# A two-block transformer kernel on one core: weight sums of the seven-product feed-forward made a step ahead, modulation loads, residual loads and stores moved

## The chip, the core and the metric

The kernel runs on one NeuronCore of a Trainium2 chip. Five engines work from queues of their own, each in the order written: PE (TensorE, matrix products), DVE (VectorE), ACT (ScalarE), POOL (GpSimd) and SP (which only issues transfers here). The metric is the device time of one execution in microseconds (us), the median of three runs.

## What is computed

Two blocks over 1024 tokens of width 1024, all in float32. The first is attention and spatial gating and then a gated feed-forward of width 2816; the second takes a modulation vector from `c`, projects, and goes through window attention, a short convolution and a mixture of 16 experts. What the change touches is the end of the first block and the modulation:

```python
xn = rms_norm(x, ffn_norm_g[l])
gate, up = jnp.split(xn @ w_gate_up[l], 2, axis=-1)
x = x + (jax.nn.silu(gate) * up) @ w_down[l]
...
mod = jnp.einsum('bd,de->be', jax.nn.silu(c), w_mod[layer]) + b_mod[layer]
mod_c = jnp.einsum('d,de->e', jax.nn.silu(c_ctx), w_mod[layer]) + b_mod[layer]
```

and, in the second block, the projection `hx @ w_in`, part of which is made in the same way.

## The kernel before

Activations stand transposed, 128 features by 1024 tokens to a tile. A float32 product is three matmuls of rounded parts (`mm3`, L65 to L67): high by high, low by high, high by low. `split` (L58, L59) makes the parts: ACT copies to the high part, DVE subtracts it to get the low one.

The hidden width of the feed-forward is 22 strips of 128 (FF = 22, `f` counts them). Strips 0 to 2 are made plainly. For `f` from 3 (NCL) on, the gate's and the up weights' column strip and the two halves of the tokens form a 2 x 2 problem that `quads` does with seven products instead of eight: seven sums of weights, seven sums of activations (`SEVX`, made beforehand), 12 matmuls each, and an evacuation `after[i]` behind each product. `after[1]` and `after[5]` end in a gate: a sum on DVE (`plus`, L326), a multiplication by the norm's factors on POOL (`times`, L1182) and SiLU on ACT (L1186). `after[4]` and `after[6]` end in `times` alone. `hidden_out` (L1137, L1138) then multiplies gate and up on DVE and stores the strip to DRAM from POOL's queue (L1139); it is put off (`flush`) to the head of the next step.

The weights come through class `Weights`. `fill` issues loads on SP (L132) into four staging tiles; `seven` lists the seven sums of a pair (a, b): a11, a12, s2 = a21 + a22 - a11, s1 = a21 + a22, a11 - a21, a12 - s2, a22. Four of these are POOL operations: `make2` makes s1 (L153) and s2 (L154), `make3` a11 - a21 (L158), `make4` a12 - s2 (L162). `conv` calls the sum, then `split`s it. `get` hands out the next prepared pair of parts and first calls `conv` until five are ready (`ahead` is 4 in the steps, 2 in the last). So what `conv` issues for product i + 4 stands, on every engine, in front of the evacuation of product i.

Beside this, the modulation: `w_mod` is 48 pieces of 512 KB (12 column strips s of 4 pieces). `mods` first sums a finished strip with matmuls against ones (`mod_sum`, L1108, L1109), then `mod_load` asks for a piece and at once accumulates it on DVE (L1097, L1099): four operations for s < 4, where both vectors are needed, two after that. One call stands at the end of each step, the rest stands between the feed-forward's halves and in the second half.

The second half multiplies the strips by `w_down` in five parts (`parts`: 5, 5, 4, 4, 4). `h_load` reads strips back into two buffers (`phr`) and `h_split` splits them; the residual `x1` is read back from `d_xs` on SP (L1249) ahead of the first part, and `columns_k` adds each product to it (L1257). The second block's projection uses `quads` again, 20 times (`quads_`, L1490 on).

```python
        def get(self):
            self.prime(1 + self.ahead)
            return self.ready.popleft()
...
            wh, wl = W.get()
            bk.append(psb.tile([P, 512], F32, name="b"))
            for k in range(4):
                mm3(bk[i], wh[:, k, :], wl[:, k, :], xh_(k), xl_(k), k == 0, k == 3)
            after[i]()
            if i in mid:
                mid[i]()
```

## Time and profile before

| | before |
|---|---|
| median of 3 runs | 3119.93 us (3118.93 to 3121.84) |
| the profiled execution | 3115.53 us |
| its span | 3113.6 us |
| mean granted clock of PE | 0.959 of full |
| PE busy | 2873.2 us, 92% |
| DVE, ACT, POOL busy | 2035.0, 1415.2, 813.1 us |

The span is the time from the first to the last instruction that the profiler records; the 1.9 us more of the execution lie around it. "Busy" of PE is modelled from the starts of the matmuls. The feed-forward in sevens goes from about 560 to 1071 us of the span, its second half to about 1350, the second block's steps of seven from about 1520 to 1890.

### The profile page before, as it was taken

To read this page: it belongs to the slowest core of one execution; us is meant where nothing else is said; L and a number is where in the kernel's file an instruction comes from. 1 tells how busy PE (TensorE), PEld (TensorE's weight loads), DVE (VectorE), ACT (ScalarE), POOL (GpSimd) and SP (SyncE) were. 2 spreads that over 40 slices of the span, in tenths; PEclk is the share of its full clock that TensorE was granted. 3 is DMA by queue.
4 is the path that set the end of the run, shared out by engine and by line. 5 is a ranking of instruction groups with operands and counts; after the bars stand their busy time and mean duration, and the time that the engine had idled before them with its cause. 6 is when DMAs were issued, how large, how long until landed. Compare 5 with 4: busy or idle time off the path is not lost.

```text
span 3113.6 us, 37585 instructions
## 1 busy us (share of the span) xinstructions
PE 2873.2 (92%) x13715; PEld 2378.2 (76%) x13715; DVE 2035.0 (65%) x2925; ACT 1415.2 (45%) x2241; POOL 813.1 (26%) x789
## 2 busy tenths in 40 slices
PE   9999999888878699999999998999999879999997
PEld 7987878666666578788788887777778758888885
DVE  4346845655555445687666663589942389999998
ACT  4346933222222211252223232488831268888886
POOL 2201312244434300033444431133221311121113
PEclk9999999988888899999999999999999989999998
DMA  5120133122222364334222236200054489999997
GB/s 193 45 72 15 47 137 109 61 81 81 81 75 74 107 210 161 123 100 144 75 86 87 86 109 240 92 14 15 35 187 153 156 291 370 377 377 372 377 377 282
DMA packets 303880, 472.76 MB, mean 152 GB/s; under 512 B 15260, under 2 KB 144000, under 8 KB 303568
## 3 DMA queue, kind: packets, MB, share of 16 engines
q1 hardware_dynamic: 282368, 395.46, 37.0%
q0 software_dynamic: 19840, 73.85, 6.8%
q8 instruction: 108, 1.77, 0.2%
q10 hardware_dynamic: 1488, 1.06, 0.1%
q14 instruction: 76, 0.62, 0.1%
HBM read 396.35 MB, written 73.96 MB: 151 GB/s over the span
## 4 chain that ended last, share of the span: by engine, by line
PE 68%; DVE 11%; issue 7%; POOL 6%; ACT 5%; DMA 2%; SPq 0%; POOLq 0%; ACTq 0%; DVEq 0%
PE b L67 19%; PE b L65 19%; PE b L66 19%; DVE acc L1099 1%; PE pt L1726 1%; DVE wl L59 1%; ACT wh L58 1%; PE b L2107 1%; POOL c L1182 1%; PE po L1756 1%; POOL wst L158 1%; POOL u L1182 1%; PE po L1757 1%; POOL ws L154 1%; POOL ws L153 1%
## 5 line engine op out<-in xcount | busy, mean ns | idle before, releaser
L59 DVE TENSOR_TENSOR wl<-wst,wh 128x1024 fp32r<-128x1024 f32 (+2 forms) x677 | 740.2, 1121 | 280.0 <-ACT wh L58 269.7
L58 ACT ACTIVATE wh<-wst 128x1024 fp32r<-128x1024 f32 (+2 forms) x677 | 610.3, 922 | 529.8 <-POOL wst L158 187.5
L65 PE MATMUL b<-wh,a 128*128 128x512 f32 x768 | 302.0, 393 | 0.2 <-ACT a L58 0.2
L66 PE MATMUL b<-wl,a 128*128 128x512 f32 x768 | 299.4, 390 | 0.8 <-DVE wl L59 0.8
L67 PE MATMUL b<-wh,a 128*128 128x512 f32 x768 | 299.4, 390 | 0.4 <-DVE a L59 0.4
L2149 POOL DMA_INDIRECT d_x<-b,idxT x15 | 65.8, 4388 | 469.9 <-DVE b L2143 469.9
L67 PEld LDWEIGHTS b<-wh,a 128*128 128x128 f32 x768 | 144.2, 188 | 30.9 <-DVE a L59 1.0
L66 PEld LDWEIGHTS b<-wl,a 128*128 128x128 f32 x768 | 144.5, 188 | 30.5 <-DVE wl L59 1.6
L65 PEld LDWEIGHTS b<-wh,a 128*128 128x128 f32 x768 | 144.5, 188 | 29.6 <-ACT a L58 0.7
L59 DVE TENSOR_TENSOR wl<-ws,wh 128x512 fp32r<-128x512 f32 x78 | 53.6, 690 | 157.3 <-ACT wh L58 157.3
L65 PE MATMUL b<-xn,wh 128*128 128x512 f32 x368 | 145.6, 396 | 5.7 <-ACT xn L58 4.8
L67 PE MATMUL b<-xn,wl 128*128 128x512 f32 x368 | 145.1, 394 | 2.6 <-DVE wl L59 2.6
L65 PE MATMUL b<-hH,wh 128*128 128x512 f32 x352 | 143.0, 406 | 4.5 <-ACT hH L58 4.5
L66 PE MATMUL b<-xn,wh 128*128 128x512 f32 x368 | 145.1, 394 | 0.5 <-DVE xn L59 0.5
L66 PE MATMUL b<-hL,wh 128*128 128x512 f32 x352 | 141.5, 402 | 1.2 <-DVE hL L59 1.2
L67 PE MATMUL b<-hH,wl 128*128 128x512 f32 x352 | 140.8, 400 | 0.0
L58 ACT ACTIVATE wh<-ws 128x512 fp32r<-128x512 f32 x78 | 47.5, 622 | 177.5 <-POOL ws L154 134.4
L65 PE MATMUL b<-t3h,wh 128*128 128x512 f32 x76 | 46.5, 611 | 87.6 <-ACT wh L58 87.6
L1099 DVE SCALAR_TENSOR_TENSOR acc<-mw,s,acc 128x512 f32<-128x512 f32 x112 | 95.7, 864 | 29.3 <-DMA mw<-in_w_mod_dram 26.5
L1707 DVE CUSTOM_DVE_ANT_0 sm<-sp,mk,nsk 128x640 f32<-128x640 f32 (+1 forms) x128 | 107.1, 838 | 0.6 <-PE sp L1696 0.3
L1744 DVE TENSOR_TENSOR pl<-pt,ph 128x512 fp32r<-128x512 f32 x152 | 102.0, 686 | 7.9 <-ACT ph L1736 7.3
L1714 ACT ACTIVATE sm<-sm,tn 128x640 f32<-128x640 f32 (+1 forms) x128 | 103.0, 805 | 0.5 <-DVE tn L1707 0.3
(668 smaller groups left out, 7622.1 us busy)
## 6 DMA issues: line engine op xcount, KB each, us to landing
wst<-in_w_exp_gate_dram SPq DMA_DIRECT2D x128, 512.0 KB, 10.8
wst<-in_w_exp_up_dram SPq DMA_DIRECT2D x128, 512.0 KB, 10.8
wst<-in_w_exp_down_dram SPq DMA_DIRECT2D x128, 512.0 KB, 10.8
wst<-in_w_in_dram SPq DMA_DIRECT2D x74, 512.0 KB, 4.0
mw<-in_w_mod_dram SPq DMA_DIRECT2D x48, 512.0 KB, 5.0
wst<-in_w_gate_up_dram SPq DMA_DIRECT2D x44, 512.0 KB, 4.1
d_h<-hr POOLq DMA_DIRECT2D x22, 512.0 KB, 2.9
hr<-d_h SPq DMA_DIRECT2D x22, 512.0 KB, 4.1
```

Of the source, the lines that this page charges most:

```text
L58: act(h, src, AF.Copy)
L59: DVE.tensor_tensor(l, src, rd(h), op=OP.subtract)
L65: PE.matmul(ps, lh, rh, start=start, stop=False)
L66: PE.matmul(ps, lh, rl, start=False, stop=False)
L67: PE.matmul(ps, ll, rh, start=False, stop=stop)
L153: POOL.tensor_tensor(s1[0], a21, a22, op=OP.add)
L1099: DVE.scalar_tensor_tensor(a, t[:, kk, :], sc, a, op0=OP.mult, op1=OP.add)
L1182: POOL.tensor_tensor(x, x, rsb[:, cs], op=OP.mult)
L1707: DVE.tensor_tensor_reduce(sms[n][:, :nk], sps.pop(n)[:, 256:256 + nk], (mk if i else mk0)[:, :nk], -0.125, nsk[:, hd:hd + 1], op0=OP.add, ...
L1714: act(sms[n][:, :nk], sms[n][:, :nk], AF.Exp, bias=m, scale=-1.0, accum_out=s)
L1744: DVE.tensor_tensor(pl, pt, rd(ph), op=OP.subtract)
L2149: nc.gpsimd.indirect_dma_start(out=d_x2, out_offset=bass.IndirectOffsetOnAxis(ap=idxT[:, e:e + 1], axis=0), in_=y, in_offset=None, compute ...
```

## The change

The three POOL operations s1, s2 and a11 - a21 become one function `make` in a queue `sums`; `presum` runs the next one. In the steps of the feed-forward it is called behind the third product for the next step's pair; in the first step, and wherever it was not called, `conv` calls it at the second sum. The second block's steps do the same. `mod_load` only loads; `mod_use` accumulates at the next call (`mod_next`). In the steps this stands behind the second product, and up to f = 10 behind the fourth as well, until 24 pieces are loaded; the other 24 are spread over the second half. The store of a strip is put off to behind the third product of the next step. The first two strips are read back in the last step, into a third buffer. The residual is read back on POOL's queue in two halves.

```diff
+        def presum(self):
+            if self.sums:
+                self.sums.popleft()()
...
-            def make2():
+            def make():
                 for x, n in ((s1, "ws1"), (s2, "ws2")):
                     x.append(self.tmp.tile([P, 512], F32, name=n).rearrange("p (k n) -> p k n", n=P))
                 POOL.tensor_tensor(s1[0], a21, a22, op=OP.add)
                 POOL.tensor_tensor(s2[0], s1[0], a11, op=OP.subtract)
-                return s2[0]
-
-            def make3():
                 POOL.tensor_tensor(a21, a11, a21, op=OP.subtract)
-                return a21
...
+            def second():
+                if not s1:
+                    self.presum()
+                return s2[0]
+            self.sums.append(make)
...
-    phr = pool(es_hr, "phr", 2)
+    phr = pool(es_hr, "phr", 3)
...
         nc.sync.dma_start(t, wsrc(w_mod_2[0], k, 2, s * 512, 512))
+        mwq.append((s, k, t))
+
+    def mod_use(s, k, t):
...
-        nc.gpsimd.dma_start(d_h[f], h)
+        stored.append(lambda: nc.gpsimd.dma_start(d_h[f], h))
...
+    def mod_next(left=0):
+        if mwq:
+            mod_use(*mwq.popleft())
+        if len(modq) > left:
+            mod_load(*modq.popleft())
+
+    def early(f):
+        if f < FF - 1:
+            W.presum()
+        else:
+            for _ in range(2):
+                h_load(next(nxt))
...
+    def mods1():
+        if modr:
+            mod_sum(modr.popleft())
+        mod_next(24)
...
-                  lambda s, b: (times(plus(s, s, b), h0), su.update(s=s)), lambda s, b: times(plus(c2, s, b), h1))
+                  lambda s, b: (times(plus(s, s, b), h0), su.update(s=s)), lambda s, b: times(plus(c2, s, b), h1),
+                  {1: mods1, 2: lambda: (stores(), early(f)), **({3: mods1} if f < NCL + 8 else {})})
             flush.append(lambda hr_=hr_, c1=c1, c2=c2, su=su, f=f: hidden_out(hr_, c1, c2, su, f))
-            mods()
-            if f == NCL:
-                mods()
...
-            if not i and not c0:
-                for k in range(KD):
-                    nc.sync.dma_start(x1[k], d_xs[k])
+            if not i:
+                for k in range(c0, c0 + 4):
+                    nc.gpsimd.dma_start(x1[k], d_xs[k])
...
-                mid={(p0, 3): (lambda p0=p0: step(p0)) for p0 in range(0, n, 2)} if c0 else ())
+                mid={(p0, c): (lambda p0=p0: step(p0)) if c0 and c == 3 else mod_next for p0 in range(0, n, 2) for c in (1, 3) if i or c0})
             if c0:
                 step(n)
-            for _ in range(4):
-                mods()
+            while modr:
+                mod_sum(modr.popleft())
...
-              lambda s, b: plus(c2, s, b))
+              lambda s, b: plus(c2, s, b), {2: W.presum})
```

On POOL, one step of the feed-forward before, from the gate multiplication of the second product to that of the next step's (c, u and s are the halves that are multiplied, ws the two sums of weights, wst a staging tile):

```order
L1182 TENSOR_TENSOR c_5117<-c_5117,s_3907 128x512
L153 TENSOR_TENSOR ws_5216<-wst 128x512
L154 TENSOR_TENSOR ws_5217<-ws_5216,wst 128x512
L1182 TENSOR_TENSOR u<-u,s_3907 128x512
L1182 TENSOR_TENSOR s<-s,s_3907 128x512
L1139 DMA d_h_4597<-hr 128x1024
L158 TENSOR_TENSOR wst<-wst 128x512
L162 TENSOR_TENSOR wst<-wst,ws_5217 128x512
L1182 TENSOR_TENSOR c_5275<-c_5275,s_3907 128x512
```

and in the changed kernel (L158 and L159 make the sums, L160 the difference, L164 the last sum, L1227 multiplies, L1151 stores):

```order
L1227 TENSOR_TENSOR c_5271<-c_5271,s_3907 128x512
L1151 DMA d_h_4597<-hr 128x1024
L158 TENSOR_TENSOR ws_5339<-wst 128x512
L159 TENSOR_TENSOR ws_5340<-ws_5339,wst 128x512
L160 TENSOR_TENSOR wst<-wst 128x512
L1227 TENSOR_TENSOR c_5272<-c_5272,s_3907 128x512
L1227 TENSOR_TENSOR u<-u,s_3907 128x512
L1227 TENSOR_TENSOR s<-s,s_3907 128x512
L164 TENSOR_TENSOR wst<-wst,ws_5340 128x512
```

The store and three weight operations now stand in one piece between the step's two first gate multiplications, and one weight operation stands at its end.

On DVE, the end of a step and the head of the next before (wl is the low part of a prepared weight, acc the modulation's accumulator, hr the hidden strip):

```order
L326 TENSOR_TENSOR s<-s,b 128x512
L1099 SCALAR_TENSOR_TENSOR acc_6342<-mw,s_70,acc_6342 128x512 x2
L1099 SCALAR_TENSOR_TENSOR acc_6345<-mw,s_70,acc_6345 128x512 x2
L1137 TENSOR_TENSOR hr<-u,c_6353 128x512
L1138 TENSOR_TENSOR hr<-s,c_6352 128x512
L59 TENSOR_TENSOR wl<-wst,wh 128x512 x2
L326 TENSOR_TENSOR c_6503<-s,b 128x512
```

and in one of the changed kernel's steps up to f = 10:

```order
L335 TENSOR_TENSOR s<-s,b 128x512
L1149 TENSOR_TENSOR hr<-u,c_5753 128x512
L1150 TENSOR_TENSOR hr<-s,c_5752 128x512
L59 TENSOR_TENSOR wl<-wst,wh 128x512 x2
L335 TENSOR_TENSOR c_5923<-s,b 128x512
L1111 SCALAR_TENSOR_TENSOR acc_5855<-mw,s_70,acc_5855 128x512 x2
L1111 SCALAR_TENSOR_TENSOR acc_5858<-mw,s_70,acc_5858 128x512 x2
L59 TENSOR_TENSOR wl<-wst,wh 128x512
L321 TENSOR_TENSOR s<-s,b 128x512
L59 TENSOR_TENSOR wl<-wst,wh 128x512
L322 TENSOR_TENSOR u<-s,b 128x512
L1111 SCALAR_TENSOR_TENSOR acc_5855<-mw,s_70,acc_5855 128x512 x2
```

The accumulations have gone from the end of the step to behind the second evacuation, and a second group of four stands behind the fourth.

## Rows read from the trace of the kernel before

**Rows 1.** Stretches: start:end, length, busy PE, PEld, DVE, ACT, POOL, clock, DMA.
```profile
600.00:627.20 27.20, 21.95 (x85) 17.28 (x84) 14.27 (x21) 5.71 (x11) 11.18 (x9) 0.88 0.24 78
1530.00:1700.00 170.00, 170.00 (x752) 140.77 (x751) 111.32 (x148) 52.45 (x87) 79.53 (x59) 1.00 0.26 81
```

**Rows 2.** Timeline, PE: start, duration; first matmul of two last products, f = 3, 21.
```profile
580.01 0.39 PE L65 MATMUL b<-t4h,wh 128*128 128x512 f32 x1
...
1065.73 0.39 PE L65 MATMUL b<-t4h,wh 128*128 128x512 f32 x1
```

**Rows 3.** The chain that ended last, 600 to 660 us: start, duration, what.
```profile
600.80 0.69 DVE c L326
...
602.83 5.67 issue
...
609.78 1.30 POOL ws L153
...
612.47 0.64 ACT wh L58
...
618.31 0.67 DVE acc L1099
...
622.72 0.61 DVE hr L1138
...
624.22 1.27 POOL wst L158
...
628.01 0.69 DVE c L326
```

**Rows 4.** Timeline, PE, one step's fifth product; in brackets idle before.
```profile
626.21 0.80 PE L65 MATMUL b<-t3h,wh 128*128 128x512 f32 x1 [5.25 <-ACT wh L58]
...
628.35 0.63 PE L66 MATMUL b<-t3l,wh 128*128 128x512 f32 x1
628.77 0.63 PE L67 MATMUL b<-t3h,wl 128*128 128x512 f32 x1
```

**Rows 5.** Waits, 600 to 1060 us: us in total, times, longest.
```profile
DVE wl L59 <- ACT wh L58: 219.1, 69, 4.7
ACT wh L58 <- POOL wst L158: 133.8, 17, 8.5
...
ACT wh L58 <- POOL ws L154: 126.0, 17, 7.4
```

**Rows 6.** Timeline, DVE and POOL, the same step.
```profile
604.04 0.69 DVE L59 TENSOR_TENSOR wl<-wst,wh 128x512 fp32r<-128x512 f32 x1 [2.56 <-ACT wh L58]
...
618.23 3.89 DVE L1099 SCALAR_TENSOR_TENSOR acc<-mw,s,acc 128x512 f32<-128x512 f32 x4
618.39 1.73 POOL L1182 TENSOR_TENSOR s<-s,s 128x512 f32<-128x512 f32 x1 [2.59 <-DVE s L326]
```

**Rows 7.** Line 1099, 570 to 1060 us: duration in ns, least/median/most.
```profile
L1099 DVE SCALAR_TENSOR_TENSOR acc<-mw,s,acc x61: 739/752/1666, 589.2 to 1050.9; 128x512 f32<-128x512 f32 x61
```

**Rows 8.** Timeline, DVE and POOL at two places in the second block's steps.
```profile
1628.19 4.06 DVE L59 TENSOR_TENSOR wl<-wst,wh 128x512 fp32r<-128x512 f32 x2 [3.51 <-ACT wh L58]
...
1630.06 1.63 POOL L154 TENSOR_TENSOR ws<-ws,wst 128x512 f32<-128x512 f32 x1
...
1832.86 0.55 POOL L1539 DMA_DIRECT2D d_ga<-g  x1 [10.78 <-ACT g L1536]
...
1833.12 0.69 DVE L59 TENSOR_TENSOR wl<-ws,wh 128x512 fp32r<-128x512 f32 x1 [1.22 <-ACT wh L58]
```

**Rows 9.** Timeline, PE, between the feed-forward's halves.
```profile
1077.05 1.87 PE L1108 MATMUL b<-ones,acc 128*128 128x1 f32 x8 [8.44 <-DVE acc L1099]
...
1086.02 0.80 PE L65 MATMUL b<-hH,wh 128*128 128x512 f32 x1 [4.49 <-ACT hH L58]
```

**Rows 10.** Waits of PE, 1066 to 1365 us.
```profile
PE b L1108 <- DVE x L1257: 7.7, 3, 3.0
```

**Rows 11.** The page's DMA issues: KB each, us to landing.
```profile
wst<-in_w_gate_up_dram SPq DMA_DIRECT2D x44, 512.0 KB, 4.1
```

More of the change, by code (lines that the diff above doesn't have):

```diff
@@ L83, in __init__ @@
             self.ready = deque()
-            self.wait, self.spare, self.tmp = [], [], None
+            self.wait, self.spare, self.sums, self.tmp = [], [], deque(), None
             if hl:
@@ L163, in make4 @@
                 return a12
-            return [(f, n, True) for f, n in ((lambda: a11, 0), (lambda: a12, 0), (make2, 0), (lambda: s1[0], 0), (make3, 0),
-                                              (make4, 0), (lambda: a22, 2))]
+            def second():
[3 more added lines that the diff above has]
+            self.sums.append(make)
+            return [(f, n, True) for f, n in ((lambda: a11, 0), (lambda: a12, 0), (second, 0), (lambda: s1[0], 0),
+                                              (lambda: a21, 0), (make4, 0), (lambda: a22, 2))]
         def conv(self):
@@ L1138, in hidden_out, with stores, h_load @@
         DVE.tensor_tensor(h[:, h0], su["s"], c1, op=OP.mult)
-        nc.gpsimd.dma_start(d_h[f], h)
+        stored.append(lambda: nc.gpsimd.dma_start(d_h[f], h))
+    mwq, stored = deque(), deque()
+    def stores():
+        while stored:
+            stored.popleft()()
+    def mod_next(left=0):
[9 more added lines that the diff above has]
+                h_load(next(nxt))
+    hraw = deque()
+    nxt = iter(range(FF))
+    def h_load(f):
+        hraw.append(phr.tile([P, T], F32, name="hr"))
+        nc.sync.dma_start(hraw[-1], d_h[f])
+    def mods1():
+        if modr:
+            mod_sum(modr.popleft())
+        mod_next(24)
     for f in range(FF):
@@ L1200, in fused @@
     W.spare.clear()
-    while modq and modq[0][1]:
-        mod_load(*modq.popleft())
-    while modr:
-        mod_sum(modr.popleft())
+    stores()
+    assert len(modq) == 24 and not modr and not mwq
     es_mo.close()
@@ L1216, in fused @@
     pmo = pool(es_mo, "pmo2", 2)
-    hraw = deque()
-    def h_load(f):
-        hraw.append(phr.tile([P, T], F32, name="hr"))
-        nc.sync.dma_start(hraw[-1], d_h[f])
     def h_split():
@@ L1227, in h_split @@
         return h, l
-    nxt = iter(range(FF))
     def h_in():
@@ L1236, in h_in @@
         return r
-    for _ in range(2):
-        h_load(next(nxt))
     hTs = []
@@ L1246, in fused @@
         for c0 in (0, 4):
-            if not i and not c0:
-                for k in range(KD):
-                    nc.sync.dma_start(x1[k], d_xs[k])
+            if not i:
+                for k in range(c0, c0 + 4):
+                    nc.gpsimd.dma_start(x1[k], d_xs[k])
             hn, nn = [], parts[i + 1][1]
             def step(p0):
-                while len(hn) < min(nn, p0 + 2 + 5 - n):
+                while len(hn) < min(nn, p0 + 5 - n):
                     hn.append(h_in())
@@ L1258, in fused @@
                 x1[c0 + c][:, hf * 512:(hf + 1) * 512], x1[c0 + c][:, hf * 512:(hf + 1) * 512], ps, op=OP.add), 2,
-                mid={(p0, 3): (lambda p0=p0: step(p0)) for p0 in range(0, n, 2)} if c0 else ())
+                mid={(p0, c): (lambda p0=p0: step(p0)) if c0 and c == 3 else mod_next for p0 in range(0, n, 2) for c in (1, 3) if i or c0})
             if c0:
                 step(n)
-            for _ in range(4):
-                mods()
+            while modr:
+                mod_sum(modr.popleft())
         hTs = hn
-    while modq or modr:
-        mods()
+    while modq or mwq:
+        mod_next()
+    while modr:
+        mod_sum(modr.popleft())
     es_mo.close()
@@ L1509, in fused @@
               lambda s, b: act(g[:, h0], plus(s, s, b), AF.Sigmoid),
-              lambda s, b: act(g[:, h1], plus(g2, s, b), AF.Sigmoid))
+              lambda s, b: act(g[:, h1], plus(g2, s, b), AF.Sigmoid), {2: W.presum})
         nc.gpsimd.dma_start(d_y[j], y)
```

## The prediction

> **What bounds the kernel now.** I read the stretches first, then the order of waits inside one of them. Where the second block projects with seven products per step, TensorE is busy for all of 170.00 us and runs 752 matmuls, 0.226 us each, at clock 1.00 [rows 1]. Where the first block's feed-forward does the same seven products, it is busy 21.95 of 27.20 us, and the granted clock is 0.88. So the second place shows what the first could be: a step has 7 x 12 = 84 matmuls, 84 x 0.2267 = 19.05 us at full clock. It takes 27.0 us on average: the last product of step f = 3 begins at 580.01, that of f = 21 at 1065.73, so 485.7 us for 18 intervals [rows 2].
>
> What takes the other 8 us is seen in the chain of waits of one step [rows 3]. Within 27.21 us (600.80 to 628.01) it hardly touches TensorE: it runs DVE, POOL, ACT, DVE, POOL and round again, because each engine takes its instructions in the order written and each evacuation stands behind a preparation for the next step. TensorE runs ahead on prepared weights and then waits 5.25 us for the fifth product's. After that wait its matmuls start 0.42 us apart instead of 0.23 [rows 4]: the records show the lower of its two clock levels, 1.2 instead of 2.4 GHz. A dozen matmuls at the lower level cost 12 x 0.2 = 2.4 us. 19.05 + 5.25 + 2.4 is 26.7, the step nearly whole. The waits say what is late: ACT waited 133.8 us for POOL's a21 difference (L158) and 126.0 us for its two sums (L154) in 17 steps [rows 5].
>
> **The change, part by part: the step.** I take the links of [rows 3] that leave the chain.
> - Sums L153 and L154 stood between the gate of the second half and the third evacuation: 609.78 to 612.47, 2.7 us. They are now made in the step before, after its third product.
> - The four modulation accumulations stood before the hidden rows were finished: 618.31 to 622.04 (L1137's 0.68 us before L1138), 3.7 us. They now stand after the second product.
> - The store: from the end of L1138 at 623.33 to L158 at 624.22, 0.9 us. It moves past the third product of the next step, where the rows are long finished.
> - L158 itself, 1.3 us, goes with the sums.
>
> Together 8.6, which leaves 18.6 us. Three things are added.
> - POOL now has store, two sums and difference in one piece (0.55 + 1.30 + 1.30 + 1.27 = 4.4 us, by [rows 3, 8]) between its two gate multiplications. POOL was free there (602.83, 5.67 us [rows 3]), so POOL is not late. DVE may be: its conversions stand in that same stretch (from 604.04 [rows 6]), and two conversions that met POOL's sums took 4.06 us instead of some 1.3, while POOL's L154 took 1.63 instead of 1.30 [rows 3, 8]. An issue of a store does not do that: a conversion that began inside one took 0.69 us [rows 8]. So the cost lies between 0 and the three operations' 3.85 us. Both sides gave way in the row, so I take the middle, 1.9 us.
> - The copy of the next step's first product overwrites the half that the last hidden multiplication reads, and it is now the next link: ACT's 0.6 us, against a POOL operation (L162, 1.3 us) that may leave the chain. Between -0.6 and +0.6; I take +0.3, since the copy is certain and the other is not.
> - The accumulations. From f = 11 on there are two a step. DVE is idle for 2.56 us in front of the conversion at 604.04 [rows 6]; two at 0.75 us [rows 7] fit: nothing. In f = 3 to 10 there are two groups of four. The first has 3.0 us for 2.56 of idle time: 0.4. The second, after the fourth product, lies on the chain: 3.0. Each group meets a POOL operation, as the group at 618.23 did (3.89 us for 3.0 [rows 6]): 2 x 0.9.
>
> So a late step costs 18.6 + 1.9 + 0.3 = 20.8 us, above TensorE's 19.05 (bounds 19.05, and 18.6 + 3.85 + 0.6 = 23.1). An early step costs 20.8 + 0.4 + 3.0 + 1.8 = 26.0, hardly less than now. The last step prepares only two products ahead; I leave it at 27. Intervals: 7 early, 10 late, 1 last: 182 + 208 + 27 = 417 against 485.7, **-69 us**.
>
> The bound of the wait for POOL is where a rule of the skill says more than a row. In 1628 to 1632 both engines were held in turn and both lost time [rows 8]. The Trainium skill, "SBUF — State Buffer", section "Who interferes with whom", says that a DVE instruction with two SBUF inputs and a GpSimd instruction that reads SBUF exclude each other for a whole instruction, the one that issues first winning. The rows agree on the exclusion, but show turns taken and not one side always losing. By the rule in full, with all 3.85 us in DVE's way, a late step would be 22.8 and an early one 28.0, the sum -35 instead of -69 and the time 3078 us.
>
> **The other parts.** Between the two halves of the feed-forward TensorE waits 8.44 us for an accumulation and 4.49 us for a hidden row [rows 9]. The accumulation is gone from there, and the first two rows are asked for in the last step, into a third buffer. What remains is their split behind the last hidden multiplications, about 6 us, an estimate: each strip is two halves of 0.64 us on ACT (L58) and two of about 0.6 on DVE (as L1138) [rows 3], so two strips take 5 us, and DVE's queue adds some 1: **-7 us**, between 0 and -13. In the second half three sums of the modulation waited 7.7 us for an evacuation [rows 10]; in the change the sums still follow the evacuations and directly follow their last accumulation, so I take nothing (between -7.7 and +5). Asking for the modulation matrix a step ahead removes waits of DVE, which sets no end there.
> At nothing: the residual's eight loads go from SP's queue to POOL's, whose issues take 0.55 us [rows 8] and stand in an idle POOL, and their tiles are needed some 27 us later by the first evacuations; without that cover they would cost 8 x 0.55 = 4.4 us. The sums made ahead in the second block's steps: TensorE is never idle there [rows 1], so nothing can be won, and the loss is covered as long as that chain stays under 19.05 us. The matrix loads now stand in front of the weight loads in SP's queue, one issue each; a pair of weights is asked for more than a step before its use.
>
> Sum: -69 - 7 = -76. The profiled execution took 3115.53 us, 4.4 less than the median of 3119.93. 3115.5 - 76 + 4.4 = **3044 us**.
>
> **Rivals.**
> - *Port and TensorE alone bind.* If the serial chain no longer closes, only two sums are left: TensorE's 19.05, and the operations that exclude each other. Early: POOL 8 x 1.28 = 10.2, DVE's nine conversions and hidden multiplications 9 x 0.61 (L1138's share in [rows 3]) and eight accumulations 8 x 0.75 [rows 7], 11.5: together 21.7. Late: 10.2 + 7.0 = 17.2, under 19.05. 7 x 21.7 + 10 x 19.05 + 27 = 369, so -117 - 7: 2996 us. For it: 170 us at full TensorE in the same kind of step [rows 1]. Against it: those steps have five or six POOL operations, these eight, and every evacuation here passes through POOL and ACT. Chance 0.14. The early step of this rival is the one that the Trainium skill's exclusion rule (same page and section) would give by itself.
> - *The POOL block lies wholly on DVE's path.* Late steps at their upper bound, 23.1, early ones as much longer, 28.3, nothing won between the halves: 198 + 231 + 27 = 456, -30: 3090 us. For it: 4.06 us for two conversions. Chance 0.17.
> - *Slower: DVE's waiting stays.* DVE waited 219.1 us for ACT in 17 steps, 12.9 us each [rows 5], and ACT's order is unchanged: its conversions still stand behind the gates. If that waiting stays whole, an early step is the old one with four more accumulations and one more turn at POOL, 27.2 + 3.9 + 1.3 = 32.4, and a late one 27.2 - 1.9 + 1.3 = 26.6: 227 + 266 + 27 = 520, +34 - 7: 3147 us. It decides once less than 27/18 = 1.5 us of the 12.9 goes. Against it: most of that waiting is ACT's own waiting for POOL, 133.8 + 126.0 us over 17 steps, and both of those operations now come a step earlier. Chance 0.06.
> - *It does not do what it says.* The sums made ahead wait for weights that have not landed, POOL's queue stands still behind them, and the step keeps its 27 us; only the 7 us are won, 3113 us, not told from no change. Chance 0.03: the loads landed 4.1 us after their issue [rows 11], which comes a step early.
>
> **How the numbers follow.** My forecast has 0.60. A measurement of this kernel can tell 0.2%, about 6 us, from no change. Faster by more: 0.60 + 0.14 + 0.17 = 0.91. Within: 0.03. Slower: 0.06. The range goes from 2985, which takes in most of the first rival, to 3100, which takes in most of the second; left out are the last two (0.09) and the edges of the first two (0.1).
>
> **What would show it.** Right: evenly spaced steps of about 21 us from f = 11 on with clock near 1.00; early steps near 26, uneven, with TensorE waiting at the sums of the modulation (L1120), which its queue now meets in the middle of a step; conversions on DVE lengthened above 1 us where POOL's three operations stand; the PE wait of 8.44 us gone. In pairs of early steps TensorE runs one at 19 us on its lead and pays in the next; if the lower clock follows such waits, a few us are added. Wrong: late steps at 19.05 (the chain is broken, first rival) or above 23; early steps above 28; or a stretch behind the feed-forward that grows by what was won.

## The result, and the profile after

The changed kernel takes 3027.24 us (median of 4 runs, 3026.69 to 3028.96) against 3120.89 us (4 runs, 3118.93 to 3122.38): a ratio of 0.9701, 95% interval 0.9684 to 0.9718, 93.7 us less. The profiled executions, 3115.53 and 3026.69 us, are 88.8 us apart. The forecast was 76 us less in the profiled execution and 3044 us for the median; of the gap of 17 us, 13 lie in the stages below and 4 in the median, which lies 0.6 us above the profiled execution here and lay 4.4 above it before.

In the changed kernel PE is busy for 2842.8 us of the span (94%), DVE for 2093.8, ACT for 1414.8 and POOL for 851.4 us.

The stages answer to [rows 1, 2]. The first matmuls of the seventh product at f = 3 and f = 21 (timeline of PE: start, duration):

```profile
580.08 0.39 PE L65 MATMUL b<-t4h,wh 128*128 128x512 f32 x1
...
990.49 0.39 PE L65 MATMUL b<-t4h,wh 128*128 128x512 f32 x1
```

That is 410.4 us for 18 intervals, against 485.7. The single ones come to 19.0, 35.7, 19.0, 32.7, 19.0, 32.4 and 19.0 us (f = 3 to 10), then 208.8 us for ten, then 24.7. Stretches of the seven early and the ten late intervals (length, busy PE, PEld, DVE, ACT, POOL, granted clock, DMA):

```profile
580.08:757.00 176.92, 151.58 (x637) 124.61 (x636) 140.36 (x169) 39.31 (x70) 88.90 (x63) 0.90 0.31 99
757.00:965.79 208.79, 199.57 (x874) 161.31 (x872) 152.34 (x188) 55.37 (x99) 123.09 (x89) 0.99 0.30 98
```

In the early steps DVE is busy 140 of 177 us, in the late ones TensorE 200 of 209. The waits in the last 17 intervals answer to [rows 5]:

```profile
DVE wl L59 <- ACT wh L58: 70.2, 42, 3.0
...
PE b L1120 <- DVE acc L1111: 23.9, 6, 6.5
ACT wh L58 <- POOL ws L159: 23.4, 17, 1.5
```

DVE's waiting for ACT's high parts fell from 219.1 us to 70.2, ACT's for POOL's weight operations from 133.8 + 126.0 to 23.4. New is TensorE's wait at the sums of the modulation. Its timeline at one of them, in an early step (in brackets the idle time before):

```profile
673.83 1.87 PE L1120 MATMUL b<-ones,acc 128*128 128x1 f32 x8 [6.24 <-DVE acc L1111]
```

Between the halves TensorE now waits 2.13 and 3.99 us where it waited 8.44, 0.76, 4.49 and 0.47 [rows 9]:

```profile
995.50 0.50 PE L65 MATMUL b<-hH,wh 128*128 128x512 f32 x1 [2.13 <-ACT hH L58]
...
999.99 0.80 PE L66 MATMUL b<-hL,wh 128*128 128x512 f32 x1 [3.99 <-DVE hL L59]
```

And in the second half (waits of PE; [rows 10] had 7.7 us, three times):

```profile
PE b L1120 <- DVE x L1288: 4.3, 1, 4.3
PE b L66 <- DVE hL L59: 4.0, 1, 4.0
PE b L1120 <- DVE acc L1111: 3.4, 1, 3.4
PE b L65 <- DVE x L1288: 2.3, 2, 1.2
```

The sums' waiting is as long as before, 4.3 + 3.4 us in two waits; 2.3 us in front of products of hidden strips, for DVE's additions to the residual (L1288), are new.

### Where the time of one step goes now

A late step on DVE, then on POOL (start, duration, operation; in brackets the idle time before and what ended it):

```profile
921.20 2.45 DVE L1111 SCALAR_TENSOR_TENSOR acc<-mw,s,acc 128x512 f32<-128x512 f32 x2
924.32 1.20 DVE L59 TENSOR_TENSOR wl<-wst,wh 128x512 fp32r<-128x512 f32 x1 [0.68 <-ACT wh L58]
925.44 0.67 DVE L321 TENSOR_TENSOR s<-s,b 128x512 f32<-128x512 f32 x1
926.04 1.18 DVE L59 TENSOR_TENSOR wl<-wst,wh 128x512 fp32r<-128x512 f32 x1
...
927.74 1.18 DVE L59 TENSOR_TENSOR wl<-wst,wh 128x512 fp32r<-128x512 f32 x1
...
929.55 0.69 DVE L335 TENSOR_TENSOR c<-s,b 128x512 f32<-128x512 f32 x1
930.16 0.68 DVE L59 TENSOR_TENSOR wl<-ws,wh 128x512 fp32r<-128x512 f32 x1
...
934.47 0.69 DVE L59 TENSOR_TENSOR wl<-ws,wh 128x512 fp32r<-128x512 f32 x1 [3.03 <-ACT wh L58]
...
937.54 1.76 DVE L1150 TENSOR_TENSOR hr<-s,c 128x512 f32<-128x512 f32 x1 [1.18 <-POOL s L1227]
```

```profile
921.36 1.74 POOL L1227 TENSOR_TENSOR c<-c,s 128x512 f32<-128x512 f32 x1 [3.16 <-DVE c L335]
...
923.65 1.31 POOL L158 TENSOR_TENSOR ws<-wst 128x512 f32<-128x512 f32 x1
925.04 1.63 POOL L159 TENSOR_TENSOR ws<-ws,wst 128x512 f32<-128x512 f32 x1
926.63 1.75 POOL L160 TENSOR_TENSOR wst<-wst 128x512 f32<-128x512 f32 x1
...
937.47 1.30 POOL L164 TENSOR_TENSOR wst<-wst,ws 128x512 f32<-128x512 f32 x1
```

The step repeats every 20.6 us. The two accumulations stand where DVE would wait for POOL's and ACT's gate anyway, and cost POOL's multiplication 0.45 us (1.74 for 1.29). The three conversions that meet POOL's L158 to L160 take 1.20, 1.18 and 1.18 us instead of 0.69, which is 1.5 us. `hidden_out`'s last multiplication, which meets L164, takes 1.76 instead of 0.69. Between the conversions stands a sum that reads PSUM (L321) and is not lengthened.

The rows give the manner of it. L1150 begins at 937.54, while L164 runs to 937.47 + 1.30 = 938.77, and ends 0.53 us after that. The conversion of 924.32 ends 0.56 us after L158 (924.96), that of 926.04 0.55 us after L159 (926.67). So whichever of the two comes second waits until the other's instruction has ended, and the price is what is left of it. The Trainium skill, "SBUF — State Buffer", section "Who interferes with whom", states that a DVE instruction with two SBUF inputs contends with a GpSimd instruction that reads SBUF. The rows agree: L59 and L1150 have both inputs in SBUF, L321 has one in PSUM.

An early step, the first and the second group of four accumulations on DVE; then POOL:

```profile
697.28 6.00 DVE L1111 SCALAR_TENSOR_TENSOR acc<-mw,s,acc 128x512 f32<-128x512 f32 x4
...
706.71 2.98 DVE L1111 SCALAR_TENSOR_TENSOR acc<-mw,s,acc 128x512 f32<-128x512 f32 x4
```

```profile
697.44 1.73 POOL L1227 TENSOR_TENSOR c<-c,s 128x512 f32<-128x512 f32 x1 [3.16 <-DVE c L335]
...
699.72 1.31 POOL L158 TENSOR_TENSOR ws<-wst 128x512 f32<-128x512 f32 x1
701.11 1.63 POOL L159 TENSOR_TENSOR ws<-ws,wst 128x512 f32<-128x512 f32 x1
```

The first group meets the gate multiplication and the two sums of weights and takes 6.00 us; the second meets nothing and takes 2.98.

### The profile page after: what moved, and what is told of

It is laid out like the page before. It is cut to its first block, busy times and chain, and to the rows that moved or that the text cites. A ratio compares the mean times of both kernels' runs of the same rounds, so it can differ in the third digit from the quotient of the medians.

```text
span 3024.9 us, 37545 instructions
## 1 busy us (share of the span) xinstructions
PE 2842.8 (94%) x13715; PEld 2366.9 (78%) x13715; DVE 2093.8 (69%) x2925; ACT 1414.8 (47%) x2241; POOL 851.4 (28%) x797
## 4 chain that ended last, share of the span: by engine, by line
PE 46%; DVE 5%; ACT 2%; DMA 2%; issue 2%; POOL 1%; POOLq 0%; SPq 0%; DVEq 0%; ACTq 0%
PE b L67 13%; PE b L66 13%; PE b L65 13%; PE pt L1760 1%; PE b L2141 1%; PE po L1790 1%; DVE pl L1778 1%; DVE wl L59 1%; DVE sm L1741 1%; PE po L1791 1%; DVE qs L1645 1%; DMA z<-d_y 1%; PE b L1983 0%; DMA ot<-d_o 0%; PE sp L1730 0%
## 5 line engine op out<-in xcount | busy, mean ns | idle before, releaser
L59 DVE TENSOR_TENSOR wl<-wst,wh 128x1024 fp32r<-128x1024 f32 (+2 forms) x677 | 768.9, 1163 | 209.3 <-ACT wh L58 201.4
L1111 DVE SCALAR_TENSOR_TENSOR acc<-mw,s,acc 128x512 f32<-128x512 f32 x112 | 114.5, 1031 | 23.8 <-DMA mw<-in_w_mod_dram 21.6
L59 DVE TENSOR_TENSOR wl<-ws,wh 128x512 fp32r<-128x512 f32 x78 | 53.5, 688 | 79.8 <-ACT wh L58 79.8
L1227 POOL TENSOR_TENSOR c<-c,s 128x512 f32<-128x512 f32 x38 | 63.2, 1662 | 148.6 <-DVE c L335 139.1
L1760 PE MATMUL pt<-ident,sm 128*128 128x128 f32 x608 | 90.8, 277 | 8.0 <-DVE qs L1645 7.6
```

The lines of the kernel that those rows point to most:

```text
L59: DVE.tensor_tensor(l, src, rd(h), op=OP.subtract)
L1111: DVE.scalar_tensor_tensor(a, t[:, kk, :], sc, a, op0=OP.mult, op1=OP.add)
L1227: POOL.tensor_tensor(x, x, rsb[:, cs], op=OP.mult)
L1760: PE.transpose(pt[:, hh * P:(hh + 1) * P], sms[4 * u + hh][:, kb * P:(kb + 1) * P], ident)
```

## The experiments

Every run is set beside the changed kernel by stages, all from the first and last matmuls of a product: "steps" from the seventh product of f = 3 to that of f = 21, "between" from there to the first matmul on a hidden strip, "half" from there to the start of the last one, "rest" from there to the span's end. The code of the last is the same in all but u_rest and no_sums; it varies by some us, more in one_group, split_group and units3. What lies before the steps varies between 575 and 581 us. The ratio of each kernel is to runs of the one before that were made beside it (medians of 3118.71 to 3120.89 us).

| kernel | median | ratio to before, 95% | steps | between | half | rest |
|---|---|---|---|---|---|---|
| before | 3120.89 | | 485.7 | 13.0 | 274.3 | 1760.5 |
| changed | 3027.24 | 0.9684 to 0.9718 | 410.4 | 5.0 | 270.0 | 1759.4 |
| u_sums | 3078.38 | 0.9841 to 0.9877 | 458.0 | 5.0 | 270.4 | 1762.9 |
| u_store | 3038.93 | 0.9720 to 0.9759 | 416.6 | 5.0 | 269.8 | 1762.6 |
| u_mods | 3044.32 | 0.9736 to 0.9769 | 422.8 | 4.9 | 271.0 | 1763.2 |
| u_h | 3042.26 | 0.9733 to 0.9768 | 410.3 | 10.5 | 277.9 | 1761.0 |
| u_rest | 3024.83 | 0.9689 to 0.9722 | 410.0 | 5.0 | 269.9 | 1759.1 |
| late_sum | 3028.18 | 0.9685 to 0.9718 | 409.2 | 5.0 | 270.2 | 1760.7 |
| no_sums | 2991.82 | 0.9574 to 0.9608 | 377.8 | 5.0 | 270.7 | 1761.0 |
| one_group | 3044.39 | 0.9739 to 0.9773 | 409.8 | 5.0 | 280.8 | 1769.0 |
| split_group | 3011.39 | 0.9639 to 0.9673 | 378.4 | 4.2 | 281.0 | 1767.2 |
| units | 3005.17 | 0.9617 to 0.9649 | 386.3 | 4.2 | 270.7 | 1762.9 |
| units3 | 3080.15 | 0.9852 to 0.9902 | 383.4 | 6.6 | 342.8 | 1766.3 |
| units_last | 3004.07 | 0.9621 to 0.9647 | 381.9 | 6.7 | 269.2 | 1764.1 |

### Undoing one part: the sums ahead, the store, the accumulations

```diff
# u_sums
 def early(f):
-        if f < FF - 1:
-            W.presum()
-        else:
+        if f == FF - 1:
# u_store, in hidden_out
-        stored.append(lambda: nc.gpsimd.dma_start(d_h[f], h))
+        nc.gpsimd.dma_start(d_h[f], h)
# u_mods
-                  {1: mods1, 2: lambda: (stores(), early(f)), **({3: mods1} if f < NCL + 8 else {})})
+                  {2: lambda: (stores(), early(f))})
             flush.append(...)
+            for _ in range(2 if f < NCL + 8 else 1):
+                mods1()
```

> The changed kernel, but the three sums of weights are made in their own step, at the second sum, as before. Chain theory (each step is one closed chain through DVE, POOL and ACT): 2.7 + 1.3 us of links come back and the 1.5 us that three conversions lose beside the sums go or move, so a step is 2 to 4 us longer, 18 steps 36 to 72 us: 3063 to 3099 us. Rival (TensorE's waits at the sums of the modulation and DVE's accumulations set the steps, the weight sums are covered): at most 15 us more, up to 3042 us.

> The changed kernel, but a strip is stored straight behind its two multiplications, at the head of the next step. Chain theory: POOL waits for the second multiplication before it may go on, 0.9 us in every step, 18 steps 16 us: 3043 us. Rival (POOL is free there and its issue is covered): 0 to 3 us more, 3027 to 3030 us.

> The changed kernel, but the modulation's accumulations (a piece asked for a step ahead, one call a step and two up to f = 10, as in the change) stand at the end of the step, ahead of the hidden multiplications. By the prediction's account 3.7 us of accumulations ahead of the hidden rows come back in each step: early steps up to 6 us longer, late ones 1.5 us, together 40 to 65 us: 3067 to 3092 us. Rival (DVE's accumulations cost the same wherever they stand, since the chain runs through DVE at both places): within 10 us of the changed kernel, 3017 to 3037 us.

The sums ahead carry most: without them the steps take 47.6 us more (2.6 each), late ones 23.8 instead of 20.6. The chain theory holds.

The store is worth 6.2 us in the steps, 0.3 each and not 0.9. The total of u_store moved by 11.7 us, of which 3 lie in the rest; its runs spread from 3034.09 to 3043.3 us, so its size stands between the two expectations. A late step of u_store, POOL and then DVE:

```profile
901.57 1.30 POOL L164 TENSOR_TENSOR wst<-wst,ws 128x512 f32<-128x512 f32 x1
```

```profile
903.57 0.69 DVE L59 TENSOR_TENSOR wl<-wst,wh 128x512 fp32r<-128x512 f32 x1 [2.29 <-ACT wh L58]
```

L164 now stands behind the store on POOL, and DVE waits 2.29 us for the copy that needs it, instead of 0.64. Against that L1150, which no longer meets L164, takes 0.69 us instead of 1.76.

The accumulations back at the end cost 12.3 us of steps (early pairs 35.1 + 19.5 us, late steps 21.2), far from the 40 to 65 of the prediction's account; the total of 3044.32 us lies 7 us above the rival's bound. DVE in a late step of u_mods shows why:

```profile
882.58 2.45 DVE L1111 SCALAR_TENSOR_TENSOR acc<-mw,s,acc 128x512 f32<-128x512 f32 x2
884.95 1.78 DVE L1149 TENSOR_TENSOR hr<-u,c 128x512 f32<-128x512 f32 x1
886.65 0.68 DVE L1150 TENSOR_TENSOR hr<-s,c 128x512 f32<-128x512 f32 x1
```

The two accumulations stand there in the time in which DVE otherwise waits 1.2 us for POOL (L1150 above, [1.18 <-POOL s L1227]); now L1149 meets L164 (1.78 us), and L1150 doesn't (0.68). Where the accumulations stood in the changed kernel, POOL's gate multiplication takes 1.29 us again.

### TensorE's stop at the sums of the modulation: late_sum

```diff
-                acc_of[s, j] = pmo.tile([P, 512], F32, name=f"acc{j}", bufs=2 - j)
+                acc_of[s, j] = pmo.tile([P, 512], F32, name=f"acc{j}", bufs=2)
...
 def mods1():
         if modr:
-            mod_sum(modr.popleft())
+            age[0] += 1
+            if age[0] > 1:
+                age[0] = 0
+                mod_sum(modr.popleft())
```

> The changed kernel, but the matmuls that sum a strip of the modulation stand two calls later than the strip's last accumulation instead of one, and both accumulators have two buffers. Chain theory (in an early step eight accumulations on DVE set the pace, TensorE's wait at L1120 is only where it shows): the 23.9 us of waiting go from there and come back at other instructions, early steps still 24 to 26 us on average, at most 8 us less: 3019 to 3027 us. Rival (the stop of TensorE in the middle of a step and the lower clock behind it are themselves the cost): 8 to 10 us less in each pair of early steps, 25 to 40 us: 2987 to 3002 us.

Waits of PE in the first ten intervals, of the changed kernel (beside the 23.9 us at L1120, all of which lie here) and of late_sum, and the stretch of each (granted clock third from the end):

```profile
PE b L67 <- DVE wl L59: 6.7, 3, 3.7
```

```profile
580.08:823.38 243.30, 212.68 (x906) 174.64 (x904) 191.25 (x230) 55.54 (x99) 124.12 (x89) 0.92 0.31 100
```

```profile
PE b L67 <- DVE wl L59: 31.6, 12, 3.8
```

```profile
578.66:820.70 242.04, 210.15 (x905) 167.75 (x904) 191.43 (x231) 56.17 (x100) 123.99 (x90) 0.97 0.31 100
```

The wait leaves L1120 and comes back, as large, at the low parts of weights (30.6 us in all before, 31.6 after). The clock rises from 0.92 to 0.97 and the ten intervals take 242.0 us instead of 243.3. TensorE waits for DVE at either place: the chain through DVE sets the pace of the early steps, and the place where TensorE stops and the lower clock behind it had together a price of 1.3 us.

### What the meeting of POOL and DVE costs: no_sums

```diff
 def make():
-                for x, n in ((s1, "ws1"), (s2, "ws2")):
-                    x.append(self.tmp.tile([P, 512], F32, name=n).rearrange("p (k n) -> p k n", n=P))
-                POOL.tensor_tensor(s1[0], a21, a22, op=OP.add)
-                POOL.tensor_tensor(s2[0], s1[0], a11, op=OP.subtract)
-                POOL.tensor_tensor(a21, a11, a21, op=OP.subtract)
+                s1.append(a22)
+                s2.append(a11)
```

> The changed kernel without the three POOL operations that make the sums of weights in the first block's feed-forward and in the second block's steps of seven: single quarters of the weights stand in for the sums, so the computation lacks them. Theory A (POOL and DVE exclude each other there): late steps fall from 20.6 to TensorE's 19.05 to 19.3 us, early ones by the 1.5 us of the conversions and the 2.5 to 3 us of the four accumulations that met the sums, to 21 to 22 us on average: 40 to 48 us less, 2979 to 2987 us. Rival (DVE's and ACT's own work sets the steps, POOL's sums lie beside it): early steps stay above 24 us and late ones above 20 us, at most 12 us less, 3015 us or more.

DVE in an early and in a late step of no_sums:

```profile
683.98 3.89 DVE L1108 SCALAR_TENSOR_TENSOR acc<-mw,s,acc 128x512 f32<-128x512 f32 x4
```

```profile
871.71 0.69 DVE L59 TENSOR_TENSOR wl<-wst,wh 128x512 fp32r<-128x512 f32 x1 [0.67 <-ACT wh L58]
...
874.12 0.68 DVE L59 TENSOR_TENSOR wl<-wst,wh 128x512 fp32r<-128x512 f32 x1
...
875.43 0.69 DVE L332 TENSOR_TENSOR c<-s,b 128x512 f32<-128x512 f32 x1
```

The same four accumulations take 3.89 us instead of 6.00, the same conversions 0.68 instead of 1.18. Late intervals fall from 20.9 us on average to 19.4, early ones from 25.3 to 23.5; 32.6 us in the steps and 35 in the time. Of the 32.6 us, 5.7 lie in the last interval (24.7 to 19.0), in whose step the changed kernel makes no sums; no run shows why.

Without the sums ACT's wait for L159 (23.4 us above) ends too, and that could be the cause instead. The rows speak against it: the conversion that needs this copy begins at 930.16 without idle time. What a late step loses lies between the first of the three conversions and the sum L335 behind the fifth product, 924.32 to 929.55 and 871.71 to 875.43: 5.23 and 3.72 us, the 1.5 us of the conversions. So theory A holds, though its size of 40 to 48 us does not: the early steps fell by 1.8 us and not by 3 to 4. In them the four accumulations still take 3.89 us and the second group stands as before.

### Where accumulations stand: one_group and split_group

```diff
# one_group
-                  {1: mods1, 2: lambda: (stores(), early(f)), **({3: mods1} if f < NCL + 8 else {})})
+                  {1: mods1, 2: lambda: (stores(), early(f)), **({3: mods1} if f in (FF - 4, FF - 3, FF - 2) else {})})
# split_group: mods1 uses a piece for j = 0 alone, mods2 for j = 1, loads the next and sums a strip
+                  {1: mods1, 2: lambda: (stores(), early(f)), 5: mods2, **({3: lambda: (mods2(), mods1())} if f in (FF - 5, FF - 4, FF - 3) else {})})
# one_group; split_group too leaves 28 pieces
-        mod_next(24)
+        mod_next(28)
# both, in the second half
-                mid={... for c in (1, 3) if i or c0})
+                mid={... for c in (1, 3)})
```

> The changed kernel, but one piece of the modulation per step, behind the second product alone (a second one only in three steps near the end, where a piece takes two accumulations); four pieces more are left to the second half, which has six more places for them. Theory A (the meeting with POOL's weight sums is the price: four accumulations behind the second product took 6.00 us, two take 2.45): 3.5 us in each of 16 steps instead of 4.7 us in 8, so the steps come to about 430 us against 410 and the kernel to 3045 us. Rival (the second group behind the fourth product is what costs, and one group fits DVE's idle time, as the prediction had it): steps of 21 us, about 380 us, 2997 us.

> As one_group, but a piece's four accumulations are parted: two behind the second product, as in the changed kernel's late steps, and two behind the sixth product, where DVE waits 3.0 us for ACT in every step; the sum of a strip stands a step later. Theory A (time on the chain counts, not DVE's sum): the two new ones fit in the wait and cost at most 0.5 us beside POOL's gate multiplications, steps of 20.6 to 21.1 us, about 380 us in all: 2993 to 3000 us. Rival (an accumulation costs what it lasts wherever it stands, as the run with them back at the end of the step suggests): 1.5 us or more per step, steps of 22 us or more, 400 us or more: 3015 us or more.

one_group's total of 3044 us is theory A's, but not for its reason: its steps take 409.8 us, neither 430 nor 380 (22.8 each); the rest of the loss lies in the second half and behind it. split_group's steps came out as theory A said, 378.4 us, 21.0 each. Its pair behind the second product takes 2.45 us in the meeting with POOL; the pair behind the sixth takes 2.88 us, inside the time in which DVE otherwise waits 3.03 us for ACT, of which 0.67 are left:

```profile
692.91 2.45 DVE L1111 SCALAR_TENSOR_TENSOR acc<-mw,s,acc 128x512 f32<-128x512 f32 x2
...
703.06 2.88 DVE L1111 SCALAR_TENSOR_TENSOR acc<-mw,s,acc 128x512 f32<-128x512 f32 x2
706.61 0.69 DVE L59 TENSOR_TENSOR wl<-ws,wh 128x512 fp32r<-128x512 f32 x1 [0.67 <-ACT wh L58]
```

The total of 3011 us lies above the 2993 to 3000 of theory A. What it gave back lies in the second half, 11 us longer with four more pieces, where TensorE waits at the sums (4.3 us in the changed kernel), and behind it:

```profile
PE b L1120 <- DVE x L1295: 17.6, 4, 11.1
```

### The rows read ahead and the residual: u_h and u_rest

```diff
# u_h
-    phr = pool(es_hr, "phr", 3)
+    phr = pool(es_hr, "phr", 2)
...
 def early(f):
-        if f < FF - 1:
-            W.presum()
-        else:
-            for _ in range(2):
-                h_load(next(nxt))
+        W.presum()
...
+    for _ in range(2):
+        h_load(next(nxt))
     hTs = []
# u_rest
-            if not i:
-                for k in range(c0, c0 + 4):
-                    nc.gpsimd.dma_start(x1[k], d_xs[k])
+            if not i and not c0:
+                for k in range(KD):
+                    nc.sync.dma_start(x1[k], d_xs[k])
# and in both calls of quads_
-              ..., {2: W.presum})
+              ...)
```

> The changed kernel, but the first two hidden strips are asked for behind the last step, into two buffers, as before. Chain theory: the second load must wait for the last strip's store, so the second row is ready about 12 us after the first matmul of the second half, where TensorE needs it after 5.4: 6 to 8 us more, 3033 to 3035 us. Rival (what was won between the halves is the accumulations alone): within 2 us of the changed kernel, 3025 to 3029 us.

> The changed kernel, but the residual is read back on SP's queue in one piece, as before, and the second block's steps make their sums of weights in their own step. By the prediction both are worth nothing: 3025 to 3030 us, the second block's steps with TensorE busy throughout. Rival for the first (SP's issues of the residual delay the hidden rows and the weights behind them): 4 us or more longer in the second half, 3031 us or more. Rival for the second (the chain of the second block's steps is near TensorE's 19.05 us and closes without the sums ahead): their stretch grows by 5 us or more, 3032 us or more.

u_h cost 15.0 us: 5.5 between the halves and 7.9 in the second half, twice the 6 to 8 expected, because two waits come instead of one. PE's timeline, and SP's (the queue that issues the loads):

```profile
1000.97 0.80 PE L65 MATMUL b<-hH,wh 128*128 128x512 f32 x1 [7.59 <-ACT hH L58]
...
1011.79 0.80 PE L65 MATMUL b<-hH,wh 128*128 128x512 f32 x1 [8.35 <-ACT hH L58]
```

```profile
985.21 10.94 SPq L132 DMA_DIRECT2D wst<-in_w_down_dram  x4
996.32 25.80 SPq L1174 DMA_DIRECT2D hr<-d_h  x7
```

The first load stands behind the four weight loads that SP issues from 985.21 to 996.15; only then do the hidden rows follow. The second waits besides for the last strip's store, as the chain theory had it: SP stands 5.4 us for it. Asked for in the last step, into a third buffer, the rows stand in front of the weights; the order and the buffer were not tried apart.

u_rest is not told from the changed kernel (3024.83 against 3027.24 us). In the second block TensorE stays busy throughout without the sums ahead:

```profile
1440.00:1610.00 170.00, 170.00 (x751) 140.77 (x750) 116.14 (x150) 53.26 (x89) 81.29 (x59) 1.00 0.26 81
```

### A faster version: units, units3, units_last

```diff
# units: one pair of accumulations a call, pieces loaded two ahead, a strip summed two calls later
+    def mods1(summed=True):
+        ...
+            mod_use(s, k, t, (part[0],))
+            part[0] = (part[0] + 1) % (1 + (s < 4))
+        ...
-                  {1: mods1, 2: lambda: (stores(), early(f)), **({3: mods1} if f < NCL + 8 else {})})
+                  {0 if f == NCL else 1: mods1, 2: lambda: (stores(), early(f)), 5: mods1, **({3: lambda: mods1(False)} if FF - 7 < f < FF - 1 else {})})
# units3
-                W.ahead = 2
+                W.ahead = 3
# units_last: units3, third pairs for FF - 8 < f < FF - 2, and behind the steps
+    W.ahead = 2
```

> A version meant to beat the change: 24 pieces of the modulation in the steps, as in the change, and its second half as it is; but accumulated two operations at a time, one pair behind the second product and one in DVE's 3.0 us wait behind the sixth in every step, a third pair behind the fourth in f = 16 to 20 alone; a strip's sum stands two pairs later. Theory A (only time on the chain counts; split_group's steps came to 378.4 us, and what it lost again lay in the second half, 281 us against 270, where it had more pieces): steps 378 + 5 x 1.5 = 386 us at most, second half 270, 2997 to 3003 us. Rival (DVE's total of accumulations in a step comes back somewhere): steps of 395 us or more, 3010 us or more.

> As units, but the last step of the feed-forward prepares three products ahead instead of two. Theory A (the last interval, 24.7 us in the changed kernel against 20.6, is long because TensorE runs out of prepared weights there): 1 to 4 us less than units. Rival (the weights of the second half have no place or have not landed, so the order makes no difference): within 1 us of units.

> As units, with two edits. The third pairs stand in f = 15 to 19, so the last strip's sum is done a step earlier; and the last step prepares three products ahead, but the second half two again (in units3 it went on with three, and ACT's conversions waited 223 us there for weight buffers that TensorE still read, with the hidden strips' splits behind them). Theory A: the last interval falls from 29.1 to 21 to 25 us and the second half stays at 270 us: 2996 to 3003 us, beside 3005 for units. Rival (preparing three in the last step already blocks the first splits of the second half): the wait moves to the start of the second half, 3003 to 3012 us.

units keeps the steps at 386.3 us and the second half at 270.7, as expected, and takes 3005.17 us, 22 less than the changed kernel and 2 above its range; its last interval, 29.1 us, is its longest. units3 shortens that to 25.5 and loses 72 us in the second half, which neither expectation had: three products are prepared ahead there too. ACT's waits in units3 from 960 to 1300 us:

```profile
ACT wh L58 <- PE b L66: 223.3, 23, 28.1
```

In units it was 145.8 us in 17 waits. units_last, which prepares two again there, brings the second half back to 269.2 us; the last interval is 24.0 us, as expected, by its two edits together, and 2.5 us return between the halves, as the rival had it. At 3004.07 us it is not told from units. Both are faster than the kernel before and the changed one.

## Why the prediction was right, and which of its terms were not

- **The bound.** "The order of waits" as a closed chain through DVE, POOL and ACT was the right reading: u_sums and late_sum both fit it, and late steps ran at 20.9 us on average (forecast 20.8), 10 intervals 208.8 us (208). Adding 5.25 us of stopping and 2.4 us of lower clock to TensorE's 19.05 described the step, but gives no prices: in late_sum the clock was 0.97 instead of 0.92 in ten intervals, and 1.3 us of 243.3 were won.
- **Sums L153, L154 and L158.** 4.0 us leave and 1.9 come back: 2.1 a step. Undoing them cost 2.6.
- **"POOL now has store, two sums and difference."** Taken as 1.9 us between 0 and 3.85; the three conversions lose 1.5. The middle was right for a wrong reason. Between the conversions DVE has sums that read PSUM, so only the remainder of each POOL operation counts. The rule of the Trainium skill, "SBUF — State Buffer", section "Who interferes with whom", is about single instructions: whichever issues first has the shared port pair for the whole of its instruction. In that form rule and rows agree; my "by the rule in full" put all of POOL's time in DVE's way, and the 22.8 us and 3078 us were worked out from this misreading.
- **The store.** 0.9 us a step was too much: 0.3. What stands behind it on POOL is delayed, L164 in u_store, but then no longer meets L1150, which gives 1.1 us back. The forecast priced the wait and not the meeting.
- **"The four modulation accumulations ... 3.7 us"** is the term that failed. The time from L1099 to L1138 was counted as removed, without the wait of DVE for POOL at the same place (1.18 us in front of L1150) that the accumulations partly fill; 2.55 us went. Undone, they cost 0.6 us in a late step and 1.3 in an early one. A late step now holds two accumulations where one before held four, so u_mods does not bring back the whole of the old price, and four at the old place were not tried alone. The three parts, each undone by itself, give back 66 of the 75 us.
- **The late step's sum** came out at 20.8 by luck: its terms were wrong by up to 2 us and cancel. DVE's step, cut at the starts of the same instructions in both traces, shows by how much:

| DVE, from start to start (in brackets where a stretch ends, before and changed) | before | changed | forecast | measured |
|---|---|---|---|---|
| from the sum behind the second product, 600.80 and 920.60, to the first conversion (604.04; 924.32) | 3.24 | 3.72 | 0 | +0.48 |
| three conversions, to the sum behind the fifth (607.77; 929.55) | 3.73 | 5.23 | +1.9 | +1.50 |
| to the conversion of a sum of weights (613.14; 930.16) | 5.37 | 0.61 | -2.7 | -4.76 |
| to the sum behind the seventh (617.63; 935.08) | 4.49 | 4.92 | 0 | +0.43 |
| to the last hidden multiplication (622.64; 937.54) | 5.01 | 2.46 | -3.7 | -2.55 |
| to the sum behind the next step's second product (628.01; 941.16) | 5.37 | 3.62 | -0.9 - 1.3 + 0.3 | -1.75 |
| the step | 27.21 | 20.56 | -6.4 | -6.65 |

The third row's 2.1 us more than forecast make up for the fifth, 1.15 us too many, and for the first and the fourth, 0.9 us left out; the first is what the two accumulations cost POOL's gate multiplication. The sixth holds L1150's meeting with L164 (1.1 us), which was left out too, and comes out near its forecast all the same. In the third, before, DVE's conversion waited for POOL's gate multiplication, both sums and ACT's copy. DVE, and then POOL, before:

```profile
607.77 0.69 DVE L326 TENSOR_TENSOR c<-s,b 128x512 f32<-128x512 f32 x1
613.14 0.69 DVE L59 TENSOR_TENSOR wl<-ws,wh 128x512 fp32r<-128x512 f32 x1 [4.68 <-ACT wh L58]
```

```profile
608.53 1.29 POOL L1182 TENSOR_TENSOR c<-c,s 128x512 f32<-128x512 f32 x1 [5.71 <-DVE c L326]
```

With the sums made a step ahead the gate (1.29 us) and the copy (0.64 us, [rows 3]) left the chain at this place too; the forecast took out the sums' 2.7 us alone.
- **The early steps.** "The first has 3.0 us for 2.56 of idle time: 0.4 ... each group meets a POOL operation: 2 x 0.9." The first group took 6.00 us for meeting three, the second 2.98 for meeting none. 176.9 us for seven against 182: the sum near, its terms not. As forecast TensorE runs one at 19 us and pays in the next.
- **The last step**, left at 27, took 24.7, and 28.4 in u_sums and 19.0 in no_sums: it goes with the sums, though in the changed kernel none are made in it. How, no run shows.
- **Between the halves** -7 was forecast and -8.0 measured, and the waits left, 2.13 + 3.99 us, are the 6 us of the forecast. But the part that matters is the early loads: without them 13.4 us come back there and in the second half, from the order of SP's queue, which the prediction did not look at in this place, and from the store that the second row waits for.
- **The second half,** "I take nothing (between -7.7 and +5)", gave -4.3. For the sums it was right: they waited 7.7 us and wait 7.7. The waits at the second row fell by 1.7 us (0.76 + 4.49 + 0.47 us before, 3.99 now), which the forecast had put between the halves, but 2.3 us of waits are new. So the gain is not in the waits: TensorE's busy time in the half fell from 260.9 to 256.1 us, with eight matmuls fewer (1128 and 1120) and at a granted clock of 0.96 instead of 0.94. What gave it the higher clock there stays open.
- **At nothing:** the residual on POOL's queue and the second block's sums ahead were nothing, as u_rest shows.
- **The rivals.** TensorE and the port alone (2996 us) did not come: late steps take 20.9 us on average while POOL's sums are there, and 19.4 without them. The slower one did not come either: DVE's waiting fell by 149 us of 219.

So -69 was -75.3 in the steps, -7 was -8.0 between the halves, 0 was -4.3 and 0 was -1.1.

## What to carry to other kernels

In a chain of in-order engines, price a moved operation by undoing it on paper at its old place: an operation that stood in another wait of its own engine gives back less than it lasts (2.55 us of 3.7), and one that others waited behind gives back more (4.76 us for 2.7). Put work of the vector engine where it waits for another engine, and not beside GpSimd's operations when both read two operands from SBUF: four accumulations in one group made steps of 22.8 us (one_group), the same four in two pairs 21.0 (split_group), where a late step of the changed kernel with one pair takes 20.6. A load that the next stage needs first belongs in front of that stage's bulk loads in the queue.

## What the runs showed of the hardware

- Of an operation of DVE with both inputs in SBUF and one of POOL's here, the second to begin waited for the end of the first: L1150 ended 0.53 us behind L164, conversions 0.55 and 0.56 us behind L159 and L158. POOL's too: L160 took 1.75 us beside a conversion, and the same difference 1.27 alone [rows 3]. Four accumulations back to back took 6.00 us beside three operations of POOL, 3.89 beside one and 2.98 alone. Sums of DVE with one input in PSUM took 0.67 us beside the same operations.
- TensorE's granted clock was 0.92 on average in ten intervals with stops of up to 6.5 us (changed kernel) and 0.97 where as much waiting was spread over 12 stops of at most 3.8 us (late_sum); the intervals took 243.3 and 242.0 us.
